# One core, a hybrid encoder block: one moving operand of 512 columns for both parts of h, and an adding transfer for the low part of some weights

## The chip, the cores and the metric

The kernel runs on one core of a Trainium2 chip. TensorE multiplies matrices into PSUM, whose eight banks hold 512 floats a partition; VectorE and ScalarE take results out of PSUM and do the elementwise work; POOL (GpSimd) does a little of it and can issue transfers; SP issues nearly all transfers. The metric is the time of one execution in microseconds on the device. Lower is better.

## The reference

The input x has 256 tokens of 2048 channels, all in float32. What is computed:

```python
h = rms_norm(x, g_pre)
proj = h @ w_in                      # 2048 x 10688: MLA, RWKV, z and gate columns
# MLA: low-rank q and kv, rotary, softmax attention over 8 heads
# RWKV-7: token shift, decays and rates, two scans (forward, backward), 16 heads of 64
u_mla  = (y_mla  * silu(z_mla))  @ w_br_mla
u_rwkv = (y_rwkv * silu(z_rwkv)) @ w_br_rwkv
merged = sigmoid(gate_mla) * u_mla + sigmoid(gate_rwkv) * u_rwkv
x = x + rms_norm(merged @ w_out, g_post)
```

The projection by `w_in` is the largest part: 16 blocks of 128 channels (k), 256 tokens, 10688 columns.

## The kernel before

**Split products.** TensorE takes the rounded type fp32r. To keep accuracy, both operands of a large product are split in a high part (rounded) and a low part (what rounding left). A product is then three matmuls: high weights by high h, high weights by low h, low weights by high h, all added in one PSUM bank. h is split once, at the start, into `hhi` and `hlo` (16 blocks of 256 columns each). Weights are split as they come.

**Chunks.** `dma_stream` loads the weights through SP in chunks of 128 x 1024 floats (512 KB: four blocks k by 256 columns) into one of three buffers `raws`. `split_stream` makes the parts: ScalarE copies `raw` to the rounded high part (line 327), VectorE subtracts (line 330) and writes the low part. There are three buffers of each (`NSPL = 3`), used in turn, so a chunk's split starts when the matmuls of the chunk three earlier are done. `mm_stream` issues the matmuls (lines 396 to 398 in `cm_task`). All matmuls of a chunk read weights as the stationary operand and h as the moving one.

**Tasks.** A projection task takes 256 columns: four chunks, two column tiles of 128, both in one PSUM bank. When its last chunk is done, an `end` generator evicts the bank: `mix` for r, k and v, `ev_z` for z, a tanh for the gates, a copy for the low-rank parts. There are 12 tasks for r, k, v, eight for z, eight gates of each branch, and four low-rank ones. Banks come from two pools, `DB` (three, for tasks) and `MB` (five, for all else).

**The scan** runs in four quads of heads. A quad's front (`front_k`, `front_v`, `front_d` for each direction) makes its operands, `chunks_of` solves and scans; each quad waits for the one before. Projection tasks are issued between its steps. After the last quad come the kv and q projections, attention, the branch projections (`um_task`, `ur_task`), and the output projection.

**Order.** The order of work on every engine is fixed when the program is built. Streams are generators that ask for an engine with a cost in microseconds (`yield ("P", cost, ready)`); a planner, `Streams.run`, grants them by estimated time and rank. The chip keeps this order on each engine, and semaphores keep the dependences. POOL's queue holds some memsets of the scan and the 16 small transfers of `front_d` (line 670).

Of the kernel before, what the change touches and what calls it, by code (L numbers as in the profile page):

```python
# [35 lines left out]
RK = 2  # L36
WARM = 12

KEEP, KEEP2 = 6, 9
# [115 lines left out]
def encoder_block_kernel(  # L155
# [51 lines left out]
    ss, rs = sb([128, 2], "ss"), sb([128, 2], "rs")  # L207
    hhi, hlo = sb([128, KT, S], "hhi", dt=F32R), sb([128, KT, S], "hlo", dt=F32R)
    raws = [sb([128, 1024], f"raw{i}") for i in range(NRAW)]
# [3 lines left out]
    W = Free(works[:-1])  # L213
    MB = Free(pps.tile([128, 512], F32, tag=f"m{i}", bufs=1, name=f"m{i}") for i in range(5))
    DB = Free(pps.tile([128, 512], F32, tag=f"d{i}", bufs=1, name=f"d{i}") for i in range(3))
    yr = sb([128, 8, 256], "yr")
# [45 lines left out]
    def add_task(parts, begin, end, ready=None, again=None):  # L262


        t = (len(chunks), len(parts), begin, end, ready, again)
        for p in parts:
            c = Chunk()
            c.load, c.pairs, c.steps = p
            c.t = c.at = 0.0
            chunks.append(c)  # L270
        tasks.append(t)
# [38 lines left out]
    def split_stream():  # L310
        i = 0
        while True:
            yield ("W", lambda: i < done["dma"])
            c = chunks[i]
            raw, c.hi, c.lo, t = raws[i % NRAW], whis[i % NSPL], wlos[i % NSPL], c.t
            if i < hold["first"]:
                yield ("W", lambda: i < done["mm"] + NSPL)
                t = max(c.t, chunks[i - NSPL].end if i >= NSPL else 0.0)
            else:
                c.hi, c.lo = hold["take"](i - hold["first"])  # L320
            beside = [p for p in c.pairs if len(p) > 3]
# [12 lines left out]
            c.at = e  # L334
            i += 1
            done["split"] = i
# [34 lines left out]
    def cm_task(src, nk, xhi, xlo, mt, wd, end, kc=4, load_fn=None, ready=None, kready=None, k_first=0,  # L371
                begin=None, pairs=None, first_alone=False):

        parts = []
        nb = (len(mt) + 1) // 2
        k0s = list(range(k_first, nk, kc))
        if first_alone:
            k0s[1:1] = [1]
        for i, k0 in enumerate(k0s):
            kc = (k0s + [nk])[i + 1] - k0  # L380

            def load(raw, k0=k0, kc=kc):
                if load_fn:
                    load_fn(raw, k0, kc)
                else:
                    nc.sync.dma_start(raw[:, 0:kc * wd].rearrange("p (k c) -> p k c", k=kc), src[:, k0:k0 + kc])

            steps = []
            for k in range(k0, k0 + kc):
                def mm(banks, hi, lo, k=k, k0=k0, kc=kc):  # L390
                    hi = hi[:, 0:kc * wd].rearrange("p (k c) -> p k c", k=kc)[:, k - k0]
                    lo = lo[:, 0:kc * wd].rearrange("p (k c) -> p k c", k=kc)[:, k - k0]
                    for i, (c, m) in enumerate(mt):
                        o = p2(banks[i // 2])[0:m, i % 2]
                        last = k == nk - 1 and (i % 2 == 1 or i == len(mt) - 1)
                        pe.matmul(o, hi[:, c:c + m], xhi(k), start=k == k_first and i % 2 == 0, stop=False)  # L396
                        pe.matmul(o, hi[:, c:c + m], xlo(k), start=False, stop=False)  # L397
                        pe.matmul(o, lo[:, c:c + m], xhi(k), start=False, stop=last)  # L398

                steps.append((len(mt) * 3 * 0.119, mm) + (((lambda k=k: kready(k)),) if kready else ()))  # L400
            parts.append((load, list(pairs(k0, kc)) if pairs else plain(kc * wd), steps))

        def take():
            b = []
            for _ in range(nb):
                b.append((yield from DB.take()))
            return b

        add_task(parts, begin or take, end, ready)
# [56 lines left out]
    def ev_second(b):  # L466
        yield ("W", lambda: len(have.get("part", ())) == 2)
        for p, m, t, B in zip(b, (96, 128), have["part"], (DB, MB)):
            yield ("D", cD(512))
            tt(w2d(t)[0:m], w2d(t)[0:m], p2(p)[0:m], ALU.add)  # L470
            B.give(p)
        yield from ev_wd(have["part"][0])
        yield from ev_ad(have["part"][1])
# [37 lines left out]
    def rwkv_tasks(Q, **kw):  # L511
        for n, nm in ((1, "k"), (0, "r"), (2, "v")):
            def end(b, n=n, nm=nm):
                t = yield from W.take(KEEP)
                yield from mix(p2(b[0]), 128, V_MU + 8 * n + 2 * Q, w2d(t))
                DB.give(*b)
                have[nm, Q] = t
            in_task(RW0 + 1024 * n + 256 * Q, end, **kw)

    def ev_z(b, o):  # L520

        z = p2(b[0])
        t = yield from W.take()
        yield ("A", cA(512), None, "exp")
        act.activation(w2d(t), z, AF.Tanh, scale=0.5)
        yield ("D", cD(512))
        stt(o, w2d(t), 1.0, z, ALU.add, ALU.mult)
        W.give(t)
        DB.give(*b)

# [7 lines left out]
    def gate_mla_task(g):  # L538
        def end(b):
            yield ("A", cA(512), None, "exp")  # L540
            act.activation(m16[:, 2 * g:2 * g + 2], p2(b[0]), AF.Tanh, scale=0.5)
            DB.give(*b)
        in_task(GM0 + 256 * g, end)

    def low_rank_task(c0, key):
        def end(b):
            t = yield from W.take(KEEP)
            yield ("A", cA(512))
            act.copy(w2d(t), p2(b[0]))
            DB.give(*b)  # L550
            have[key] = t
# [107 lines left out]
    def front_d(Q, d):  # L659
# [7 lines left out]
        raw = krw[d] if Q == 0 else (yield from W.take())  # L667
        e = yield ("G", 2.1, O.free["P"] if Q == 0 else None)
        for i, w in enumerate(((w2_f, a2_f), (w2_b, a2_b))[d]):
# [373 lines left out]
    def wkv_task(g):  # L1043
        wkv_v = wkv_b.rearrange("(k p) c -> p k c", p=128)

        def begin():
            if g == 0:
                yield ("W", lambda: quads[3].done and len(MB.tiles) > 1)
                DB.give(MB.tiles.pop())
                att["kT"] = sb([128, 2, 8, 256], "g16", dt=F32R)  # L1050
# [11 lines left out]
            a = yield from DB.take()  # L1062
            b = yield from DB.take()
            return a, b

# [37 lines left out]
    def wq_task(g):  # L1103
        wq_v = wq_b.rearrange("(k p) (h c) -> p k h c", p=128, c=192)

        def begin():
            a = yield from DB.take()
            b = yield from DB.take()
            return a, b

# [46 lines left out]

        add_task(parts, begin, end, lambda: have["qhl"][1] if "qhl" in have else None)

# [91 lines left out]
    def gate_rwkv_task(g):  # L1251
# [22 lines left out]

        in_task(GR0 + 256 * g, end)

# [34 lines left out]
    def out_task(n, wo_v=w_out.rearrange("(k p) c -> p k c", p=128)):  # L1311
        N = slice(512 * n, 512 * n + 512)

        def begin():
            if n == 0:
# [3 lines left out]
                MB.tiles.clear()  # L1319
            a = yield from DB.take()  # L1320
            b = yield from DB.take()
            return a, b

# [30 lines left out]
        def gain(b, t):  # L1354
            yield ("D", cD(512))
            tt(fin["og"][:, t, N], b[t], fin["gpb"][:, N], ALU.mult)
            DB.give(b[t])

        def end(b):
            for t in range(2):  # L1360
                yield from square(b, t)
                yield from gain(b, t)
            fin["left"] -= 2
            if n == 2:
# [159 lines left out]

    def begin_second():
        a = yield from DB.take()
        b = yield from MB.take()
        return a, b
# [3 lines left out]
    cm_task(None, KT, *HX, LORA, 512, ev_second, kc=2, pairs=pairs_first, load_fn=load_first, kready=lambda k: have.get(("h", k)),  # L1532
            k_first=UN, begin=begin_second)
    rwkv_tasks(0, kready=lambda k: have.get(("h", k)))
# [119 lines left out]
```

## Time and profile before

| | |
|---|---|
| median of 3 runs | 873.82 us (873.45 to 874.61) |
| the profiled execution | 872.72 us, its span 870.9 |
| TensorE busy | 848.3 us (97%) |
| VectorE busy | 659.3 us (76%) |
| ScalarE busy | 501.1 us (58%) |
| POOL busy | 30.7 us (4%) |
| DMA queue of SP | 135.16 MB, 52.4% of 16 engines' span |

The span runs from the first to the last instruction of one profiled execution; what lies around it is 1.8 us. Busy times are of that execution alone. Matmuls overlap in the pipeline, so that the durations of single matmuls add up to more than TensorE's busy time: from one start to the next is what a matmul takes of the stream.

### The profile page before, as it was taken

To read this page: it belongs to the slowest core of one execution; us is meant where nothing else is said; L and a number is where in the kernel's file an instruction comes from. 1 tells how busy PE (TensorE), PEld (TensorE's weight loads), DVE (VectorE), ACT (ScalarE), POOL (GpSimd) and SP (SyncE) were. 2 spreads that over 40 slices of the span, in tenths; PEclk is the share of its full clock that TensorE was granted. 3 is DMA by queue.
4 is the path that set the end of the run, shared out by engine and by line. 5 is a ranking of instruction groups with operands and counts; after the bars stand their busy time and mean duration, and the time that the engine had idled before them with its cause. 6 is when DMAs were issued, how large, how long until landed. Compare 5 with 4: busy or idle time off the path is not lost.

```text
span 870.9 us, 19398 instructions
## 1 busy us (share of the span) xinstructions
PE 848.3 (97%) x8112; PEld 810.0 (93%) x8112; DVE 659.3 (76%) x1082; ACT 501.1 (58%) x797; POOL 30.7 (4%) x66
## 2 busy tenths in 40 slices
PE   9999999999999999999999999999999999999996
PEld 8999999988899998999889999899999999998884
DVE  5878898868987878988789878775867556775554
ACT  6777644487544578354776445586766434444442
POOL 4110000000000000000000000000000000000000
PEclk9999999999999999999999999999999999999999
DMA  9565646633376523565423665346444675555553
GB/s 286 169 181 148 176 129 187 169 99 90 101 212 177 161 68 97 158 193 169 132 76 96 195 188 152 98 149 186 136 128 147 232 257 190 176 193 193 194 195 119
DMA packets 123528, 139.41 MB, mean 160 GB/s; under 512 B 6704, under 2 KB 110512, under 8 KB 123056
## 3 DMA queue, kind: packets, MB, share of 16 engines
q1 hardware_dynamic: 121664, 135.16, 52.4%
q0 software_dynamic: 768, 1.57, 0.6%
q10 hardware_dynamic: 1008, 1.44, 0.5%
q8 instruction: 63, 1.03, 0.5%
q14 instruction: 25, 0.20, 0.1%
HBM read 136.05 MB, written 2.10 MB: 159 GB/s over the span
## 4 chain that ended last, share of the span: by engine, by line
PE 73%; DVE 14%; ACT 8%; issue 2%; DMA 2%; DVEq 0%; ACTq 0%
PE d L396 16%; PE d L398 16%; PE d L397 15%; DVE wlo L330 4%; PE m L1334 2%; PE m L1335 2%; PE m L1336 2%; ACT whi L327 2%; DVE work L191 2%; PE m L398 2%; PE m L396 2%; PE m L397 2%; PE d L1335 1%; PE d L1334 1%; PE d L1336 1%
## 5 line engine op out<-in xcount | busy, mean ns | idle before, releaser
L327 ACT CAST whi<-raw 128x1024 fp32r<-128x1024 f32 (+3 forms) x252 | 252.8, 1004 | 254.2 <-PE d L397 155.1
L330 DVE TENSOR_TENSOR wlo<-raw,whi 128x1024 fp32r<-128x1024 f32 (+3 forms) x250 | 292.4, 1171 | 125.0 <-ACT whi L327 123.4
L396 PE MATMUL d<-hhi,whi 128*128 128x256 f32 (+1 forms) x1296 | 375.1, 289 | 0.0
L398 PE MATMUL d<-hhi,wlo 128*128 128x256 f32 (+1 forms) x1296 | 366.5, 283 | 2.3 <-DVE wlo L330 2.3
L397 PE MATMUL d<-hlo,whi 128*128 128x256 f32 (+1 forms) x1296 | 366.2, 283 | 0.0
L396 PEld LDWEIGHTS d<-hhi,whi 128*128 128x128 f32 (+1 forms) x1296 | 246.8, 190 | 4.5
L398 PEld LDWEIGHTS d<-hhi,wlo 128*128 128x128 f32 (+1 forms) x1296 | 246.9, 190 | 2.7 <-DVE wlo L330 2.7
L397 PEld LDWEIGHTS d<-hlo,whi 128*128 128x128 f32 (+1 forms) x1296 | 247.1, 191 | 0.1
L191 DVE TENSOR_TENSOR work<-work,work 128x512 f32<-128x512 f32 (+5 forms) x64 | 38.8, 612 | 3.9 <-ACT work L575 1.2
L191 DVE TENSOR_TENSOR u<-u,tmp 128x30 f32<-128x30 f32 (+7 forms) x120 | 29.9, 250 | 3.0
L191 DVE TENSOR_TENSOR tmp<-u 128x30 f32<-128x30 f32 (+7 forms) x120 | 29.8, 249 | 2.9
L396 PE MATMUL d<-b,whi 128*128 128x256 f32 x96 | 27.1, 282 | 0.0
L398 PE MATMUL d<-b,wlo 128*128 128x256 f32 x96 | 27.1, 282 | 0.0
L398 PE MATMUL d<-ar,wlo 128*128 128x256 f32 x96 | 27.0, 281 | 0.0
L397 PE MATMUL d<-work,whi 128*128 128x256 f32 x96 | 26.9, 280 | 0.0
L397 PE MATMUL d<-ar,whi 128*128 128x256 f32 x96 | 26.9, 280 | 0.0
L396 PE MATMUL d<-ar,whi 128*128 128x256 f32 x96 | 26.8, 279 | 0.0
L1334 PE MATMUL m<-whi,hhi 128*128 128x512 f32 x60 | 23.3, 389 | 0.0
L1335 PE MATMUL m<-wlo,hhi 128*128 128x512 f32 x60 | 23.3, 389 | 0.0
L1336 PE MATMUL m<-whi,hlo 128*128 128x512 f32 x60 | 23.3, 389 | 0.0
L191 DVE TENSOR_TENSOR g<-m,mask 128x512 f32<-128x512 f32 x32 | 20.6, 686 | 0.0
L797 PE MATMUL m<-ar,u 64*128 64x128 f32 x256 | 19.2, 285 | 0.3 <-DVE g L191 0.3
(334 smaller groups left out, 1487.3 us busy)
## 6 DMA issues: line engine op xcount, KB each, us to landing
raw<-in_w_in_dram SPq DMA_DIRECT2D x160, 512.0 KB, 3.9
raw<-in_w_out_dram SPq DMA_DIRECT2D x32, 512.0 KB, 3.6
raw<-in_w_br_mla_dram SPq DMA_DIRECT2D x16, 512.0 KB, 4.0
raw<-in_w_br_rwkv_dram SPq DMA_DIRECT2D x16, 512.0 KB, 3.3
raw<-in_mla_wkv_b_dram SPq DMA_DIRECT2D x8, 512.0 KB, 3.9
raw<-in_mla_wq_b_dram SPq DMA_DIRECT2D x8, 384.0 KB, 3.3
raw<-in_w_in_dram SPq DMA_DIRECT2D x7, 384.0 KB, 5.3
g<-in_x_dram SPq DMA_DIRECT2D x2, 1024.0 KB, 6.9
```

What stands on the lines that cost most here:

```text
L191: dve.tensor_tensor(out=o, in0=a, in1=b, op=op)
L327: act.copy(dst(c.hi), src(raw))
L330: eng.tensor_tensor(out=dst(c.lo), in0=src(raw), in1=dst(c.hi).bitcast(F32), op=ALU.subtract)
L396: pe.matmul(o, hi[:, c:c + m], xhi(k), start=k == k_first and i % 2 == 0, stop=False)
L397: pe.matmul(o, hi[:, c:c + m], xlo(k), start=False, stop=False)
L398: pe.matmul(o, lo[:, c:c + m], xhi(k), start=False, stop=last)
L797: pe.matmul(m[:, q * 128:q * 128 + 128], z.kb[R64[h], d, j, q], z.ar[d][R64[h], j, q], start=q == 0, stop=q == 3)
L1334: pe.matmul(banks[t], hhi[:, k, T], hi, start=k == 0, stop=False)
L1335: pe.matmul(banks[t], hhi[:, k, T], lo, start=False, stop=False)
L1336: pe.matmul(banks[t], hlo[:, k, T], hi, start=False, stop=k == KT - 1)
```

## The change

`hhi` and `hlo` become the two halves of one tile `hh`. In 32 of the projection tasks the high weights then meet both halves in one matmul of 512 columns, which fills a bank, and the low weights meet the high half in one of 256 columns, which adds into the bank's first half. Each column tile has a bank of its own, so a task takes two, and its eviction first adds the halves (`total`). The eight recurrent gates (`both=None`), the low-rank starts, and all products behind them keep the three matmuls. The pools become four and four banks.

In one chunk of three (`i % 3 == 1`), from the end of quad 0's second front until quad 3 is done, ScalarE writes the negated rounded weights to the low part, POOL issues a transfer that adds the weights from DRAM to it, and ScalarE writes the high part; VectorE does nothing for that chunk. The planner counts the transfer as landing 4.0 us after its issue, and gives the next load on SP 1.46 us for it.

```diff
+ACC, LAND = 3, 4.0
...
-    hhi, hlo = sb([128, KT, S], "hhi", dt=F32R), sb([128, KT, S], "hlo", dt=F32R)
+
+    hh = sb([128, 2, KT, S], "hh", dt=F32R)
+    hhi, hlo = hh[:, 0], hh[:, 1]
...
-    MB = Free(pps.tile([128, 512], F32, tag=f"m{i}", bufs=1, name=f"m{i}") for i in range(5))
-    DB = Free(pps.tile([128, 512], F32, tag=f"d{i}", bufs=1, name=f"d{i}") for i in range(3))
+    MB = Free(pps.tile([128, 512], F32, tag=f"m{i}", bufs=1, name=f"m{i}") for i in range(4))
+    DB = Free(pps.tile([128, 512], F32, tag=f"d{i}", bufs=1, name=f"d{i}") for i in range(4))
+
+    def take_banks(n):
+        b = []
+        for _ in range(n):
+            b.append((yield from DB.take()))
+        return b
...
             for (n, src, dst, *_) in c.pairs[:len(c.pairs) - len(beside)]:
+                if c.again and i % ACC == 1 and ("front", 0, 1) in have and not quads[3].done:
+
+                    e = yield ("A", cA(n), t)
+                    act.activation(dst(c.lo), src(raw), AF.Copy, scale=-1.0)
+                    e = yield ("G", 0.65, e)
+                    c.again(c.lo)
+                    O.free["S"] = max(O.free["S"], O.free["G"]) + 1.46
+                    yield ("A", cA(n), t)
+                    act.copy(dst(c.hi), src(raw))
+                    e += LAND
+                    continue
...
+            def again(lo, k0=k0, kc=kc):
+                gp.dma_start(lo[:, 0:kc * wd].rearrange("p (k c) -> p k c", k=kc), src[:, k0:k0 + kc], accum_op=ALU.add)
...
                     for i, (c, m) in enumerate(mt):
+                        if both:
+
+                            o = p2(banks[i])[0:m]
+                            pe.matmul(o, hi[:, c:c + m], both(k), start=k == k_first, stop=False)
+                            pe.matmul(o[:, 0], lo[:, c:c + m], xhi(k), start=False, stop=k == nk - 1)
+                            continue
...
-                steps.append((len(mt) * 3 * 0.119, mm) + (((lambda k=k: kready(k)),) if kready else ()))
...
+                steps.append((len(mt) * (0.347 if both else 3 * 0.119), mm) + (((lambda k=k: kready(k)),) if kready else ()))
...
     def in_task(c0, end, w=256, mt=PAIR, **kw):
+        kw.setdefault("both", lambda k: hh[:, :, k])
         cm_task(w_in_v[:, :, c0:c0 + w], KT, *HX, mt, w, end, **kw)
+
+    def total(b, o):
+
+        for i in range(2):
+            yield ("A", cA(256) - 0.05)
+            act.copy(o[:, i], p2(b[i])[:, 1])
+        for i in range(2):
+            yield ("D", cD(256))
+            tt(o[:, i], p2(b[i])[:, 0], o[:, i], ALU.add)
+            DB.give(b[i])
...
                 t = yield from W.take(KEEP)
-                yield from mix(p2(b[0]), 128, V_MU + 8 * n + 2 * Q, w2d(t))
-                DB.give(*b)
+                yield from total(b, w2d(t))
+                yield from mix(w2d(t), 128, V_MU + 8 * n + 2 * Q, w2d(t))
...
-        z = p2(b[0])
+        yield from total(b, o)
...
-            act.activation(m16[:, 2 * g:2 * g + 2], p2(b[0]), AF.Tanh, scale=0.5)
-            DB.give(*b)
+            act.activation(o, o, AF.Tanh, scale=0.5)
...
-            yield ("A", cA(512))
-            act.copy(w2d(t), p2(b[0]))
-            DB.give(*b)
+            yield from total(b, w2d(t))
...
-        in_task(GR0 + 256 * g, end)
+        in_task(GR0 + 256 * g, end, both=None)
```

## Rows read from the trace of the kernel before

**Rows 1.** The page: span, busy time of each engine, and the granted clock in 40 slices.

```profile
span 870.9 us, 19398 instructions
PE 848.3 (97%) x8112; PEld 810.0 (93%) x8112; DVE 659.3 (76%) x1082; ACT 501.1 (58%) x797; POOL 30.7 (4%) x66
PEclk9999999999999999999999999999999999999999
```

**Rows 2.** The page: shares of the chain that ended last, by engine and by line.

```profile
PE 73%; DVE 14%; ACT 8%; issue 2%; DMA 2%; DVEq 0%; ACTq 0%
PE d L396 16%; PE d L398 16%; PE d L397 15%; DVE wlo L330 4%; PE m L1334 2%; PE m L1335 2%; PE m L1336 2%; ACT whi L327 2%; DVE work L191 2%; PE m L398 2%; PE m L396 2%; PE m L397 2%; PE d L1335 1%; PE d L1334 1%; PE d L1336 1%
```

**Rows 3.** Busy time by engine, summed over 88 to 558 us (stretch, then engines).

```profile
sum 470.00, PE 459.86 PEld 441.65 DVE 397.90 ACT 273.81 POOL 12.80; mean PE 51.10 PEld 49.07 DVE 44.21 ACT 30.42 POOL 1.42
```

**Rows 4.** Timeline of TensorE in the projection: start, us, line, op, tiles.

```profile
639.81 0.28 PE L397 MATMUL d<-hlo,whi 128*128 128x256 f32 x1
643.89 0.28 PE L398 MATMUL d<-hhi,wlo 128*128 128x256 f32 x1
```

**Rows 5.** Timeline of TensorE in the output projection.

```profile
799.78 0.39 PE L1334 MATMUL m<-whi,hhi 128*128 128x512 f32 x1
805.90 0.39 PE L1334 MATMUL d<-whi,hhi 128*128 128x512 f32 x1
```

**Rows 6.** Groups by line: shapes, count | busy us, mean ns | idle before.

```profile
L396 PE MATMUL d<-hhi,whi 128*128 128x256 f32 (+1 forms) x1296 | 375.1, 289 | 0.0
L1086 PE MATMUL d<-whi,b 128*128 128x256 f32 x32 | 9.0, 281 | 0.0
```

**Rows 7.** The split's subtraction, 88 to 558 us: count, ns least/median/most.

```profile
L330 DVE TENSOR_TENSOR wlo<-raw,whi x124: 1201/1225/1228, 87.6 to 555.1; 128x1024 fp32r<-128x1024 f32 x124
```

**Rows 8.** Groups by line and shape: ScalarE's cast, VectorE's subtraction.

```profile
L327 ACT CAST whi<-raw 128x1024 fp32r<-128x1024 f32 x227 | 238.0, 1049 | 247.2 <-PE d L397 155.1 <-PE d L1336 24.5 <-DMA raw<-in_w_in_dram 15.1
L330 DVE TENSOR_TENSOR wlo<-raw,whi 128x1024 fp32r<-128x1024 f32 x227 | 277.5, 1224 | 114.4 <-ACT whi L327 112.7
```

**Rows 9.** POOL's own transfers: duration of an issue in ns, and issue to landing.

```profile
L670 POOL DMA_DIRECT2D work<-in_rwkv_w_f_dram x4: 512/512/645, 17.5 to 351.6; - x4
DMA to landing us min/median/max: 2.1/3.1/4.8
```

**Rows 10.** Timeline of ScalarE in a steady stretch.

```profile
497.20 1.05 ACT L327 CAST whi<-raw 128x1024 fp32r<-128x1024 f32 x1 [1.83 <-PE d L397]
500.08 1.05 ACT L327 CAST whi<-raw 128x1024 fp32r<-128x1024 f32 x1 [1.83 <-PE d L397]
```

**Rows 11.** The subtraction's instructions alone, by stretch; DMA share, GB/s at the end.

```profile
118.00:176.00 58.00, 24.48 (x21) 0.00 (x0) 1.00 0.63 174
248.00:298.00 50.00, 20.82 (x17) 0.00 (x0) 1.00 0.65 182
364.00:418.00 54.00, 22.02 (x18) 0.00 (x0) 1.00 0.65 183
486.00:536.00 50.00, 20.99 (x18) 0.00 (x0) 1.00 0.65 180
```

**Rows 12.** Weight loads issued by one line: us from issue to landing.

```profile
DMA to landing us min/median/max: 3.1/3.8/6.3
```

**Rows 13.** Transfers by issue: count, KB each, median us to landing.

```profile
raw<-in_w_in_dram SPq DMA_DIRECT2D x160, 512.0 KB, 3.9
g<-in_x_dram SPq DMA_DIRECT2D x2, 1024.0 KB, 6.9
yr<-in_g_post_dram SPq DMA_DIRECT2D x1, 1024.0 KB, 4.8
work<-in_rwkv_w_f_dram POOLq DMA_DIRECT2D x4, 96.0 KB, 2.8
```

**Rows 14.** Groups by line and shape: 256 columns out of PSUM.

```profile
L1205 ACT COPY work<-m 128x256 f32<-128x256 f32 x16 | 5.8, 377 | 1.8 <-PE m L1203 1.8
L191 DVE TENSOR_TENSOR tmp<-m,z 128x256 f32<-128x256 f32 x8 | 3.4, 425 | 1.1 <-PE m L941 0.9
```

More of the change, by code (lines that the diff above doesn't have):

```diff
@@ L267, in add_task @@
             c = Chunk()
-            c.load, c.pairs, c.steps = p
+            c.load, c.pairs, c.steps, c.again = *p, *([None] * (4 - len(p)))
             c.t = c.at = 0.0
@@ L371, in cm_task @@
     def cm_task(src, nk, xhi, xlo, mt, wd, end, kc=4, load_fn=None, ready=None, kready=None, k_first=0,
-                begin=None, pairs=None, first_alone=False):
+                pairs=None, first_alone=False, both=None):
         parts = []
-        nb = (len(mt) + 1) // 2
         k0s = list(range(k_first, nk, kc))
@@ L398, in mm @@
                         pe.matmul(o, lo[:, c:c + m], xhi(k), start=False, stop=last)
-                steps.append((len(mt) * 3 * 0.119, mm) + (((lambda k=k: kready(k)),) if kready else ()))
[L401 to L409, printed above, removed]
+                steps.append((len(mt) * (0.347 if both else 3 * 0.119), mm) + (((lambda k=k: kready(k)),) if kready else ()))
+            parts.append((load, list(pairs(k0, kc)) if pairs else plain(kc * wd), steps, None if load_fn else again))
+        add_task(parts, lambda: take_banks(len(mt) if both else (len(mt) + 1) // 2), end, ready)
     HX = (lambda k: hhi[:, k]), (lambda k: hlo[:, k])
@@ L467, in ev_second @@
         yield ("W", lambda: len(have.get("part", ())) == 2)
-        for p, m, t, B in zip(b, (96, 128), have["part"], (DB, MB)):
+        for p, m, t in zip(b, (96, 128), have["part"]):
             yield ("D", cD(512))
             tt(w2d(t)[0:m], w2d(t)[0:m], p2(p)[0:m], ALU.add)
-            B.give(p)
+            DB.give(p)
         yield from ev_wd(have["part"][0])
@@ L520, in ev_z @@
     def ev_z(b, o):
-        z = p2(b[0])
+        yield from total(b, o)
         t = yield from W.take()
         yield ("A", cA(512), None, "exp")
-        act.activation(w2d(t), z, AF.Tanh, scale=0.5)
+        act.activation(w2d(t), o, AF.Tanh, scale=0.5)
         yield ("D", cD(512))
-        stt(o, w2d(t), 1.0, z, ALU.add, ALU.mult)
+        stt(o, w2d(t), 1.0, o, ALU.add, ALU.mult)
         W.give(t)
-        DB.give(*b)
     def z_task(c0, key):
@@ L539, in end @@
         def end(b):
+            o = m16[:, 2 * g:2 * g + 2]
+            yield from total(b, o)
             yield ("A", cA(512), None, "exp")
-            act.activation(m16[:, 2 * g:2 * g + 2], p2(b[0]), AF.Tanh, scale=0.5)
-            DB.give(*b)
+            act.activation(o, o, AF.Tanh, scale=0.5)
         in_task(GM0 + 256 * g, end)
@@ L547, in end @@
             t = yield from W.take(KEEP)
-            yield ("A", cA(512))
-            act.copy(w2d(t), p2(b[0]))
-            DB.give(*b)
+            yield from total(b, w2d(t))
             have[key] = t
@@ L667, in front_d @@
         raw = krw[d] if Q == 0 else (yield from W.take())
-        e = yield ("G", 2.1, O.free["P"] if Q == 0 else None)
+        e = yield ("G", 1.2, O.free["P"] if Q == 0 else None)
         for i, w in enumerate(((w2_f, a2_f), (w2_b, a2_b))[d]):
@@ L1047, in begin @@
             if g == 0:
-                yield ("W", lambda: quads[3].done and len(MB.tiles) > 1)
-                DB.give(MB.tiles.pop())
+                yield ("W", lambda: quads[3].done)
                 att["kT"] = sb([128, 2, 8, 256], "g16", dt=F32R)
@@ L1061, in begin @@
                     tt(t[R64[i]], kr[R64[i]], att["kr"][0][R64[i]].bitcast(F32), ALU.subtract)
-            a = yield from DB.take()
-            b = yield from DB.take()
-            return a, b
+            return (yield from take_banks(2))
         parts = []
@@ L1104, in wq_task @@
         wq_v = wq_b.rearrange("(k p) (h c) -> p k h c", p=128, c=192)
[L1106 to L1109, printed above, removed]
         parts = []
@@ L1156, in end @@
                 O.add(head(g, i), 1, O.free["D"])
-        add_task(parts, begin, end, lambda: have["qhl"][1] if "qhl" in have else None)
+        add_task(parts, lambda: take_banks(2), end, lambda: have["qhl"][1] if "qhl" in have else None)
     def half_split(src, hi, lo, n):
@@ L1319, in begin @@
                 MB.tiles.clear()
-            a = yield from DB.take()
-            b = yield from DB.take()
-            return a, b
+            return (yield from take_banks(2))
         parts, more = [], []
@@ L1356, in gain @@
             tt(fin["og"][:, t, N], b[t], fin["gpb"][:, N], ALU.mult)
-            DB.give(b[t])
         def end(b):
@@ L1362, in end @@
                 yield from gain(b, t)
+                DB.give(b[t])
             fin["left"] -= 2
@@ L1523, in pairs_first @@
                ("kr", 0 if k0 < 2 else 2 if k0 < 8 else 8))
[L1525 to L1528, printed above, removed]
     LORA = [(0, 96), (128, 96), (256, 128), (384, 128)]
@@ L1532, in encoder_block_kernel @@
     cm_task(None, KT, *HX, LORA, 512, ev_second, kc=2, pairs=pairs_first, load_fn=load_first, kready=lambda k: have.get(("h", k)),
[L1533 removed]
+            k_first=UN)
     rwkv_tasks(0, kready=lambda k: have.get(("h", k)))
```

## The prediction, made before the changed kernel was run

> **What bounds the kernel now.** I read the page's busy times first, then the chain that ended last, then the engines in stretches of the span. TensorE is busy for 848.3 of the 870.9 us and holds its upper clock, 2.4 GHz, in every slice [rows 1]; the chain is 73% TensorE, and the three lines of the projection's matmuls carry most of it [rows 2]. So a microsecond off TensorE's own stream counts nearly whole, and one taken off VectorE or ScalarE counts only where TensorE waits for it. Between 88 and 558 us, which is where the scan of the four quads runs, TensorE is busy for 459.86 of 470 us [rows 3]: at most 10.1 us of waiting can be won there. VectorE has 397.90 us in it (85%), ScalarE 273.81 (58%).
>
> **Part 1, the long moving operand.** Today each (k, column tile) of a projection is three matmuls of 256 columns; afterwards it is one of 512 and one of 256. What counts is start to start, since the durations in the profile overlap. In the projection, 34 steps lie between the two rows at 639.81 and 643.89 us: 4.08/34 = 0.1200 us each [rows 4]. In the output projection the matmuls have 512 columns: 27 steps from 799.78 to 805.90 us, 6.12/27 = 0.2267 us [rows 5]. At 2.4 GHz these are 288 and 544 cycles: the columns and 32 more, whatever the length. A group thus goes from 3 x 0.1200 = 0.3600 to 0.2267 + 0.1200 = 0.3467 us, 13.3 ns less. The change reaches 32 tasks (12 for r, k, v; 8 gates of the attention branch; 8 z; 4 low rank) x 16 k x 2 tiles = 1024 groups. The eight recurrent gates keep the old form, 8 x 32 = 256 groups, and the two low-rank starts their 64; together these are 1344, of which 1296 stand in the first row of [rows 6] and the rest write banks of the other pool. Term: 1024 x 13.3 ns = **-13.65 us**, all on TensorE's stream. A moving operand in two pieces (the two halves lie apart in SBUF) is to be seen in the kv projection, where two runs of 128 columns cost a mean of 281 ns against 289 for the plain one [rows 6], so I charge nothing for the stride. Bounds: 0, if each half pays the 32 cycles again, and 13.65.
>
> The Trainium skill speaks against this term: "TensorE: Matmul & The Clock Gate", section "Back-to-back issue gap", gives N/2.4 + 2.5 ns at the full clock, so only 2.5 ns a matmul could be saved by joining two. By it the term would be 1024 x 2.5 ns = -2.6 us; the 13.3 ns that this trace shows over the columns [rows 4, 5] disagree, and I go by the trace.
>
> **Part 2, the adding transfer.** For one chunk in three, from the end of the first front to the end of the last quad, ScalarE writes the negated rounded weights into the low tile, POOL issues a transfer that adds the weights from DRAM, and ScalarE then writes the high part. Between 88 and 558 us 124 chunks are split [rows 7], so some 41 are taken. Removed: 41 VectorE subtractions of 1.224 us = 50 us. Added: 41 ScalarE passes of 1.049 us = 43 us [rows 8], and 41 issues on POOL of 0.512 us, the duration of its small transfers there [rows 9], 21 us on an engine that is busy for 30.7 of 870.9 [rows 1]. More descriptors may make an issue longer than that.
>
> What TensorE feels is when the low part is ready. There are three buffers of split weights. A cast starts when the matmuls of the chunk three earlier end, and in the steady stretches every 2.88 us [rows 10]: that is one chunk of 24 matmuls at 0.1200. From the cast's start TensorE still has two chunks to do. After the change a chunk is 8 x 0.3467 = 2.77 us, so the first low matmul is due 2 x 2.77 + 0.23 (its high matmul) = 5.77 us after ScalarE starts. ScalarE's pass takes 1.05, and I allow 0.1 for the hand-overs, which leaves **4.6 us** from POOL's issue to landing. Today the subtraction takes 1.2 of it. That tight spacing holds in four stretches with 21 + 17 + 18 + 18 = 74 chunks in 212 us [rows 11], 25 of them with an adding transfer. The other 50 chunks are spread over 258 us (5.2 us each), so their 16 transfers have some 9 us and cost nothing.
>
> How long the adding transfer takes, no row shows. From below: the 512 KB weight loads, in the same runs of 1 KB, land in 3.1/3.8/6.3 us (least, median, most) [rows 12, 13]; that is 0.8 us early, and costs 0. From above: such a transfer reads its bytes from two places, 1 MB in all, and the slowest 1 MB load took 6.9 us [rows 13], which is 2.3 us late, 25 x 2.3 = 58 us. The other 1 MB load, issued amid the branch projections' weight loads, took 4.8 us [rows 13]. I take that one: same size, same company. It is 0.2 us late, 25 x 0.2 = **+5.0 us**. The gain of part 1 is gone at 13.65/25 = 0.55 us late, that is at 5.15 us to landing. POOL's own small transfers (96 KB [rows 13]) take 2.1/3.1/4.8 us [rows 9], so the fixed part on that queue is no shorter than on SP's.
>
> The Trainium skill's "DMA: Bandwidth & Descriptors", section "Anatomy of one DMA", puts a transfer from POOL's queue at 2.0 us plus its bytes at 436 GB/s. That would be an estimated 3.2 us for 512 KB and 4.4 for 1 MB, both inside the 4.6, and the stall would be 0; the 96 KB rows at a median of 3.1 [rows 9] are above what the rule gives them (2.2), so I don't rely on it.
>
> The extra 41 x 0.5 MB share the 16 DMA engines with the weight loads, which keep them 63 to 65% busy in the tight stretches [rows 11]. A weight load has some 6 us (three chunks, 8.3 us, less about 2.1 until ScalarE has read the buffer twice) against a median of 3.8, so it stays covered; it costs if a load's time grows by half. On POOL the issues stand in one queue with the memsets of the scan's tiles, which wait for a tile's last reader, and an issue behind one is late by that wait. Those memsets belong to the scan's wide stretches, where the transfer has its 9 us: 0, unless such a wait passes 4 us.
>
> **Part 3, banks and evictions.** A task now fills two banks, and the two halves are summed on the way out: 2 ScalarE copies of 256 columns at 0.377 us and 2 VectorE additions at 0.425 [rows 14], for 32 tasks 24 us on ScalarE and 27 on VectorE. TensorE covers them: four banks are two tasks, so the eviction has the 11.1 us of the next task for 1.6 us of work. Should that cover go, each late eviction stalls TensorE by what it is late; behind it in ScalarE's and VectorE's queues stand the next chunk's split and the scan's steps. The scan has four banks in place of five. VectorE ends with 50 - 27 = 23 us less, ScalarE with 43 + 24 = 67 us more (58% becomes 73% of those 470 us). Both ways this acts only through the 10.1 us of waiting: it can give back at most that, and I let it cost as much at the other end. I take 0, since one engine gains about where the other loses.
>
> **Sum.** The profiled execution took 872.72 us (span 870.9 and 1.8 around it): 872.72 - 13.65 + 5.0 + 0 = 864.1. The median of the runs shown, 873.82, is 1.1 above it, so I forecast **865.2 us**.
>
> **Rivals.** (a) *The transfer lands late.* The adding transfer moves twice the bytes and meets weight loads that already hold the DMA engines 65% [rows 11]; at 5.6 us it is 1.0 late, 25 us: 872.72 - 13.65 + 25 + 1.1 = 885. It decides from 5.15 us on. For it: the 6.9 us row, and single loads of 6.3 [rows 12, 13]. Against it: 3.8 in the median, and 4.8 for 1 MB. (b) *The join saves nothing*, each half paying its 32 cycles: 872.72 + 5.0 + 1.1 = 879. Against it: the kv projection's split operand [rows 6]. The skill's rule above points the same way, with most of the gain missing. (c) *The evictions eat it*: two banks a task and 15 points more on ScalarE cost the 10 us that I allowed: 865.2 + 8 to 10 = 873 to 875, about no change. For it: VectorE at 85% [rows 3], where the sums queue. (d) *Everything lands in time* (under 4.6 us), and a relieved VectorE gives back some 4 of the 10.1 us of waiting: 872.72 - 13.65 - 4 + 1.1 = 856.
>
> **How the numbers follow.** Forecast 0.48 (own range 860 to 870), (d) 0.14, (a) 0.22, (b) 0.06, (c) 0.10. 0.2% is 1.75 us, about what a measurement of this kernel can tell from no change. Faster by more: 0.48 + 0.14 = 0.62, less 0.01 for the forecast's edge: 0.61. Within it: (c) for the most part, 0.10. Slower: (a) + (b) + the rest, 0.29. The range, 855 to 890, leaves out the lower edge of (d), about 0.05, and the part of (a) with landings past 5.8 us, about 0.12.
>
> **What would show it.** Part 1: the projection's matmuls step by 0.227 and 0.120 us, and 1024 of each stand in the groups. Part 2: some 42 transfers on POOL's queue into the low tiles; their median time to landing against 4.6 us, and TensorE idle before the low matmul, released by that transfer, at some 5 us in total (under 3 is (d), over 14 is (a)). Part 3: TensorE waits for VectorE's sums nowhere by more than a few us in total. The forecast is wrong if landings pass 5.15 us in the tight stretches, or if the 512-column step there is above 0.227.

## The result, and the profile after

The changed kernel takes **999.57 us** (median of 4 runs, 998.31 to 1000.71) against 873.63 of the kernel before, run beside it: a ratio of 1.144 [1.142, 1.146]. The forecast was 865.2, in a range to 890: faster was forecast and slower measured, and the time is off by 134 us.

The page, the answer to [rows 1]:

```profile
span 996.5 us, 17533 instructions
PE 887.8 (89%) x7088; PEld 785.5 (79%) x7088; DVE 639.1 (64%) x1109; ACT 553.5 (56%) x894; POOL 78.9 (8%) x103
PEclk9999988899988989998997988899999999999998
```

The span is 125.6 us longer. TensorE is idle for 996.5 - 887.8 = 108.7 us of the span, against 22.6 before: 86.1 more. It is also *busy* for 39.5 us more, with 1024 matmuls fewer. The line of clocks shows what goes with it: it was 9 in every slice, and now 8 stands in many, with a 7. The groups of instructions show where the idle time lies (to be held against [rows 6, 8, 9]):

```profile
L420 PE MATMUL d<-hh,whi 128*128 128x512 f32 x1024 | 400.1, 427 | 0.0
L421 PE MATMUL d<-hh,wlo 128*128 128x256 f32 x1024 | 305.6, 298 | 80.5 <-DMA wlo<-in_w_in_dram 78.3
L339 ACT ACTIVATE wlo<-raw 128x1024 fp32r<-128x1024 f32 x37 | 39.2, 1059 | 137.4 <-PE d L421 135.3
L409 POOL DMA_DIRECT2D wlo<-in_w_in_dram x37 | 47.9, 1295 | 508.6 <-ACT wlo L339 425.2
```

Of the 86.1 us, 80.5 stand before one line, the low weights' matmul, and 78.3 of these end with the adding transfer. The waits put that at 25 times, 4.7 us the longest:

```profile
PE d L421 <- DMA wlo<-in_w_in_dram: 78.3, 25, 4.7
```

The transfers by issue, from issue to landing (median), and the line's least, median and most, against [rows 12, 13]:

```profile
raw<-in_w_in_dram SPq DMA_DIRECT2D x160, 512.0 KB, 4.3
wlo<-in_w_in_dram POOLq DMA_DIRECT2D x37, 512.0 KB, 7.7
...
DMA to landing us min/median/max: 5.9/7.7/9.3
```

The adding transfer lands 7.7 us after its issue; not one lands within the 4.6 us that a steady stretch leaves. The timeline of TensorE around one such stall:

```profile
584.85 0.40 PE L420 MATMUL d<-hh,whi 128*128 128x512 f32 x1
...
586.97 0.40 PE L420 MATMUL d<-hh,whi 128*128 128x512 f32 x1
590.85 0.39 PE L421 MATMUL d<-hh,wlo 128*128 128x256 f32 x1 [3.48 <-DMA wlo<-in_w_in_dram]
591.07 0.40 PE L420 MATMUL d<-hh,whi 128*128 128x512 f32 x1
...
592.60 0.63 PE L420 MATMUL d<-hh,whi 128*128 128x512 f32 x1
593.02 0.41 PE L421 MATMUL d<-hh,wlo 128*128 128x256 f32 x1
593.24 0.63 PE L420 MATMUL d<-hh,whi 128*128 128x512 f32 x1
...
595.07 0.40 PE L420 MATMUL d<-hh,whi 128*128 128x512 f32 x1
...
600.72 0.40 PE L420 MATMUL d<-hh,whi 128*128 128x512 f32 x1
```

Before the stall, six groups take 2.12 us. After it, from 592.60 to 593.24, one takes 0.64, nearly twice as long: TensorE is at 1.2 GHz. It is back at 2.4 GHz at 595.07, from where 16 groups take 5.65 us, 0.353 each. The seven groups from 591.07 to 595.07 take 4.00 us in place of 2.47, so a stall of 3.5 us costs 1.5 us more behind it. Over the span the mean granted clock is 0.948, which is 0.052/0.5 x 996.5 = 104 us at the lower level, and half of it, at most 52 us, is work done late:

```profile
core 0: 996.5 us, clock 0.948
```

So the 125.6 us are +86.1 idle and +39.5 busy. The join takes some 7 off the busy time (below), which leaves 47 for the lower clock, under its bound of 52. That 47 is what is left over, not a measurement; two experiments below (the adding transfers alone, and the stalls filled) show 33 to 37 us of it.

### The profile page after: what moved, and what is told of

It is laid out like the page before. It is cut to its first block, busy times and chain, and to the rows that moved or that the text cites. A ratio compares the mean times of both kernels' runs of the same rounds, so it can differ in the third digit from the quotient of the medians.

```text
span 996.5 us, 17533 instructions
## 1 busy us (share of the span) xinstructions
PE 887.8 (89%) x7088; PEld 785.5 (79%) x7088; DVE 639.1 (64%) x1109; ACT 553.5 (56%) x894; POOL 78.9 (8%) x103
## 3 DMA queue, kind: packets, MB, share of 16 engines
q1 hardware_dynamic: 121664, 135.16, 45.4%
q0 software_dynamic: 20304, 20.97, 13.5%
## 4 chain that ended last, share of the span: by engine, by line
PE 38%; DMA 8%; ACT 4%; DVE 3%; issue 1%; POOL 0%; DVEq 0%; ACTq 0%
DMA wlo<-in_w_in_dram 6%; PE d L425 6%; PE d L427 5%; PE d L426 5%; PE d L420 3%; PE d L421 2%; PE m L1358 1%; PE m L1356 1%; PE m L1357 1%; PE d L1356 1%; PE d L1358 1%; PE d L1357 1%; ACT wlo L339 1%; DMA work<-in_rwkv_a_f_dram 1%; PE m L1236 1%
## 5 line engine op out<-in xcount | busy, mean ns | idle before, releaser
L420 PE MATMUL d<-hh,whi 128*128 128x512 f32 x1024 | 400.1, 427 | 0.0
L421 PE MATMUL d<-hh,wlo 128*128 128x256 f32 x1024 | 305.6, 298 | 80.5 <-DMA wlo<-in_w_in_dram 78.3
L351 DVE TENSOR_TENSOR wlo<-raw,whi 128x1024 fp32r<-128x1024 f32 (+3 forms) x213 | 247.4, 1162 | 193.3 <-ACT whi L348 192.5
L421 PEld LDWEIGHTS d<-hh,wlo 128*128 128x128 f32 x1024 | 210.0, 205 | 88.9 <-DMA wlo<-in_w_in_dram 86.4
L420 PEld LDWEIGHTS d<-hh,whi 128*128 128x128 f32 x1024 | 208.1, 203 | 49.3
L425 PE MATMUL d<-hh,whi 128*128 128x256 f32 (+1 forms) x320 | 93.0, 291 | 0.0
L427 PE MATMUL d<-hh,wlo 128*128 128x256 f32 (+1 forms) x320 | 90.5, 283 | 0.0
L426 PE MATMUL d<-hh,whi 128*128 128x256 f32 (+1 forms) x320 | 90.4, 282 | 0.0
L409 POOL DMA_DIRECT2D wlo<-in_w_in_dram x37 | 47.9, 1295 | 508.6 <-ACT wlo L339 425.2
L425 PEld LDWEIGHTS d<-hh,whi 128*128 128x128 f32 (+1 forms) x320 | 60.3, 188 | 0.9
L426 PEld LDWEIGHTS d<-hh,whi 128*128 128x128 f32 (+1 forms) x320 | 60.3, 189 | 0.1
L427 PEld LDWEIGHTS d<-hh,wlo 128*128 128x128 f32 (+1 forms) x320 | 60.3, 188 | 0.0
```

Source lines behind the costliest of these rows:

```text
L409: gp.dma_start(lo[:, 0:kc * wd].rearrange("p (k c) -> p k c", k=kc), src[:, k0:k0 + kc], accum_op=ALU.add)
L420: pe.matmul(o, hi[:, c:c + m], both(k), start=k == k_first, stop=False)
L421: pe.matmul(o[:, 0], lo[:, c:c + m], xhi(k), start=False, stop=k == nk - 1)
```

## The experiments

The order of work is planned anew for every kernel, so each experiment also moves work a little. Here is the same account for all of them, from each page: idle is span less TensorE's busy time, the last column is span x (1 - clock)/0.5. All columns but the median belong to the one profiled execution; with ScalarE's half it took 889.1 us, and with four split buffers 934.94.

| kernel | median us | span | idle | busy | mean clock | us at 1.2 GHz |
|---|---|---|---|---|---|---|
| before | 873.63 | 870.9 | 22.6 | 848.3 | 0.998 | 3 |
| changed | 999.57 | 996.5 | 108.7 | 887.8 | 0.948 | 104 |
| join alone | 915.30 | 912.7 | 54.2 | 858.5 | 0.963 | 68 |
| adding transfers alone | 990.01 | 986.3 | 101.4 | 884.9 | 0.954 | 91 |
| stalls filled | 978.73 | 976.4 | 45.8 | 930.6 | 0.987 | 25 |
| plain transfers | 904.80 | 900.8 | 45.4 | 855.4 | 0.987 | 23 |
| four split buffers | 919.50 to 936.71 | 933.2 | 62.0 | 871.2 | 0.964 | 67 |
| evictions added | 899.39 | 896.7 | 42.2 | 854.5 | 0.983 | 30 |
| ScalarE's half of them | 884.05 | 887.3 | 31.1 | 856.2 | 0.982 | 32 |
| two banks held | 875.31 | 873.7 | 24.4 | 849.3 | 0.998 | 3 |
| both of these | 912.68 | 911.5 | 49.6 | 861.9 | 0.975 | 46 |

**The adding transfers alone.** The kernel before with that hunk of the change; three matmuls a group, five and three banks.

```diff
+                    act.activation(dst(c.lo), src(raw), AF.Copy, scale=-1.0)
...
+                    c.again(c.lo)
```

> The kernel before with the adding transfers alone: three matmuls of 256 columns, five and three banks, old evictions. My theory: 873.6 + 25 stalls of 3.3 - 0.2 us (78) + what the clock loses (126 + 13.65 - 81 = 58) = 1009, between 995 and 1020. Rival (the join makes the stalls, since it shortens the cover by 0.2 us a chunk and takes a bank from the scan): under 950.

Measured: 990.01 (988.06 to 994.38), ratio 1.133 [1.130, 1.137], below the expected range. One line holds the idle time:

```profile
L414 PE MATMUL d<-hhi,wlo 128*128 128x256 f32 (+1 forms) x1296 | 384.5, 297 | 81.0 <-DMA wlo<-in_w_in_dram 80.2
```

The transfers alone make +116 us, by the same wait. The stalls came out as expected, and the miss is in the clock: TensorE is busy for 36.6 us more than before, with the same matmuls, where 58 had been expected.

**The transfers by themselves.** A kernel that does only transfers of 512 KB, four of each kind, here without the plain ones of SP and the plain ones in runs of 4 KB: plain from POOL, adding into float32, plain into the rounded type, adding into the rounded type, the same in runs of 4 KB, and adding beside 18 loads on SP's queue.

```diff
+        gp.dma_start(k4(t), short(n))
+        gp.dma_start(k4(t), short(n), accum_op=ALU.add)
+        gp.dma_start(k4(r), short(n))
+        gp.dma_start(k4(r), short(n), accum_op=ALU.add)
+        gp.dma_start(r, w[:, n, 0:1024], accum_op=ALU.add)
```

> Transfers alone, no other work (the output is not the reference's): 512 KB into one tile, four of each kind one after the other: SP plain, POOL plain, POOL adding into float32, POOL converting into fp32r, POOL adding into fp32r, POOL adding with runs of 4 KB, POOL plain with runs of 4 KB, and at last POOL adding into fp32r beside 18 weight loads on SP. My theory (the add itself is slow: 101 ns a packet of 1 KB against 46 plain, and a longer issue): adding lands in 5.9 us alone and 7 to 8 us beside loads, plain from POOL in about 4. Rival (only the company of the weight loads makes it late): under 4.6 us alone. Open, no forecast: whether the conversion or the addition costs it, and what longer runs do.

Measured, by line, in that order (duration of an issue, then issue to landing):

```profile
L95 POOL DMA_DIRECT2D plain<-in_w_in_dram x4: 748/760/919, 15.9 to 29.8; - x4
DMA to landing us min/median/max: 4.2/4.3/4.4
...
L97 POOL DMA_DIRECT2D plain<-in_w_in_dram x4: 1267/1284/1313, 34.3 to 53.0; - x4
DMA to landing us min/median/max: 5.9/5.9/6.1
...
L100 POOL DMA_DIRECT2D rounded<-in_w_in_dram x4: 740/748/767, 60.3 to 74.1; - x4
DMA to landing us min/median/max: 4.1/4.2/4.5
...
L102 POOL DMA_DIRECT2D rounded<-in_w_in_dram x4: 1258/1273/1293, 78.5 to 97.2; - x4
DMA to landing us min/median/max: 5.9/5.9/6.0
...
L104 POOL DMA_DIRECT2D rounded<-in_w_in_dram x4: 835/844/867, 103.4 to 120.9; - x4
DMA to landing us min/median/max: 5.5/5.5/5.8
...
L114 POOL DMA_DIRECT2D rounded<-in_w_in_dram x4: 1268/1278/1308, 144.0 to 171.4; - x4
DMA to landing us min/median/max: 8.0/9.0/9.8
```

The addition costs 1.6 to 1.7 us with nothing beside it (5.9 against 4.3 in float32, against 4.2 rounded), a third of that in the issue; rounding costs nothing (5.9 either way with the addition). The company of weight loads adds some 3 us (9.0 against 5.9), above the 7 to 8 that were expected; those loads landed in 7.4 us themselves, against 3.7 alone, so they stood closer than in the kernel. So 4.6 us was out of reach in any case.

**Plain transfers in the changed kernel.** The low part then holds the whole weight.

```diff
-    gp.dma_start(lo[...], src[:, k0:k0 + kc], accum_op=ALU.add)
+    gp.dma_start(lo[...], src[:, k0:k0 + kc])
```

> The changed kernel with the one word for the addition taken out of its transfers: POOL issues plain transfers of the same weights into the low part, in the same places and order (so the low part holds the whole weight). Alone, such a transfer landed in 4.2 us and its issue took 0.75, against 5.9 and 1.27 for the adding one. Theory (the addition makes the transfer late): landing at a median of 5 to 6, the 81 us of stalls before the low matmuls fall to 20 to 45, time 930 to 965. Rival (any second transfer beside the weight loads is late): landing 7 or more, time 985 to 1000.

Measured: 904.80 (900.25 to 907.54), ratio 1.034 [1.030, 1.038], 95 us faster than the changed kernel for one word:

```profile
L421 PE MATMUL d<-hh,wlo 128*128 128x256 f32 x1024 | 291.0, 284 | 18.7 <-DMA wlo<-in_w_in_dram 16.2
...
DMA to landing us min/median/max: 4.2/4.6/8.8
```

The landing falls to a median of 4.6 and is just the room; the stalls fall to 18.7. Landing, stalls and time all lie below the expected ranges, so the addition counts for more than I thought. The rival, that any second transfer is late, is out. The queues of POOL, in the changed kernel and in this one (packets, MB, share of 16 engines' span), show where:

```profile
q0 software_dynamic: 20304, 20.97, 13.5%
...
q0 software_dynamic: 20304, 20.97, 10.3%
```

For the same packets and bytes that is 0.135 x 16 x 996.5/20304 = 0.106 us a packet with the addition and 0.073 without. That 904.8 lies below the join alone, at 915, would fit VectorE's 37 subtractions less: the scan's last matmul ends at 571.7 us here and at 614.8 there.

**The stalls filled.** Before each of the 25 late matmuls stand matmuls by zero (5 to 39, from the length of the stall), so that TensorE isn't idle.

```diff
+                            for _ in range(now.pop("fill", 0)):
+                                pe.matmul(o[:, 0]..., hi[:, c:c + m], zero..., start=False, stop=False)
```

> The changed kernel, with matmuls by zeros put into the 25 stalls: ahead of the first low matmul of each chunk that waited, as many of 256 columns as fill its wait but 0.2 us. They add nothing to the result; the stalls stay as long. My theory (idle TensorE falls to 1.2 GHz and runs the next microseconds at half speed, worth some 50 to 60 us): 940 to 952 us and a mean granted clock over 0.99. Rival (the clock falls for another reason, or its loss hides in the stalls): within 5 us of 999.6.

Measured: 978.73 (978.18 to 980.31). The clock rose to 0.987, not to above 0.99, and only 21 us came back, which lies in neither range. The account shows both sides. TensorE's idle time fell by 62.9 us, its busy time rose by 42.8, and the zero matmuls take up to 79.7 of it:

```profile
L428 PE MATMUL d<-zero,whi 128*128 128x256 f32 x631 | 79.7, 283 | 0.0
```

So some 80 us of fill stand for 63 of waiting, 17 too many, and the other matmuls were busy for 79.7 - 42.8 = 37 us less (33 if a zero matmul counts 0.120 us). That is what the clock gave back; at 104 - 25 = 79 us fewer at 1.2 GHz its bound is 39. The time alone shows 21, since the fill was too long.

**Four split buffers.** The changed kernel with one buffer more of either part, 15 work tiles in place of 19, and 7.7 and 1.28 us as prices in the plan.

```diff
-NW, NRAW, NSPL = 19, 3, 3
+NW, NRAW, NSPL = 15, 3, 4
```

> The changed kernel with four buffers of split weights in place of three (four work tiles fewer, 15 in place of 19, to make room), and the order of the work written for an issue of 1.28 us and a landing of 7.7. A chunk more between cast and matmul is 2.77 us more room: 7.4 in place of 4.6. Theory (the stalls are the landing less the room): those before the low matmuls fall from 81 us to 5 to 20, the low clock goes with them, and VectorE's 50 us of relief shorten the scan against the join alone: 885 to 915. Rival (the transfers load the DMA engines and so make the weight loads late whatever the room, or fewer work tiles cost the scan): 930 or more.

Measured: 919.50 in one of four runs (clock 0.983) and 933.93 to 936.71 in the others (0.964 to 0.968), too wide apart for an interval. The profile is of one at 934.94.

```profile
L421 PE MATMUL d<-hh,wlo 128*128 128x256 f32 x1024 | 293.8, 287 | 20.8 <-DMA wlo<-in_w_in_dram 20.8
...
DMA to landing us min/median/max: 5.9/7.7/10.2
```

The same landing, a chunk more of room, and 20.8 us of stalls in place of 80.5, all in 11 waits: this bears out that the wait is the landing less the room. By the medians 25 x (7.7 - 7.4) = 7.5 us would be left; single landings took up to 10.2. The time came out above what was expected in all four runs. Whether the four work tiles cost the rest was not tried.

**The join alone.** The changed kernel without the transfers.

```diff
-ACC, LAND = 3, 4.0
+ACC, LAND = 1 << 20, 4.0
```

> The changed kernel without its adding transfers: every low part is made by VectorE again; the joined matmuls, the banks and the evictions stay. My theory (the late transfers and what they do to TensorE's clock are the whole loss, the join gives its 13.65 us): 873.6 - 13.65 = 860, between 857 and 864. Rival (two banks a task and the added eviction work cost as well): 870 or more, with TensorE idle before the projection's matmuls.

Measured: 915.30 (913.19 to 916.58), ratio 1.047 [1.044, 1.049]. My theory fell: a change that saves TensorE's work costs 41 us (874.36 beside it). The join does what it says, with less gain: in a steady stretch (ScalarE's casts, as in [rows 10])

```profile
127.57 1.05 ACT L348 CAST whi<-raw 128x1024 fp32r<-128x1024 f32 x1
130.39 1.05 ACT L348 CAST whi<-raw 128x1024 fp32r<-128x1024 f32 x1 [1.77 <-PE d L420]
```

a chunk takes 2.82 to 2.83 us and not 2.77, against 2.88 before: some 6 to 7 ns a group, about 7 us in all and not 13.65. But late in the scan TensorE has too little to do (stretch and its length, busy us of TensorE, its weight loads, VectorE, ScalarE, POOL, granted clock, DMA share, GB/s):

```profile
475.00:500.00 25.00, 18.26 (x154) 14.44 (x148) 16.93 (x27) 17.69 (x35) 3.11 (x7) 0.80 0.34 93
500.00:525.00 25.00, 15.80 (x78) 12.89 (x79) 14.10 (x21) 5.74 (x11) 0.00 (x0) 0.52 0.00 1
525.00:550.00 25.00, 25.00 (x190) 23.98 (x189) 19.37 (x39) 12.38 (x17) 0.00 (x0) 1.00 0.62 164
...
575.00:600.00 25.00, 14.99 (x282) 12.88 (x280) 15.53 (x23) 11.78 (x22) 0.00 (x0) 0.66 0.25 81
600.00:625.00 25.00, 17.91 (x279) 15.75 (x278) 16.84 (x36) 11.31 (x27) 0.61 (x2) 0.80 0.01 2
```

From 500 to 525 us hardly a byte is loaded, and TensorE is at 1.2 GHz for nearly all of it. From 483 to 518.57 us no projection chunk is worked on, only the scan's own matmuls, and then the first one has waited for VectorE:

```profile
518.57 0.80 PE L420 MATMUL d<-hh,whi 128*128 128x512 f32 x1 [5.67 <-DVE work L193]
```

That is the sum that empties a bank. Between 449.71 and 518.10 us VectorE makes no such sum, while two tasks are multiplied, the last of their matmuls at 483.00: they hold all four banks. The program's order has their evictions that late, behind steps of the scan; why it does was not tried. Either the added evictions, or the two banks a task, or both must have brought it about.

**Evictions added, without the join.** The kernel before, and in the 32 tasks:

```diff
+        for i in range(2):
+            act.copy(o[:, i], p2(b[0])[:, i])
+        for i in range(2):
+            tt(o[:, i], p2(b[0])[:, i], o[:, i], ALU.max)
```

> The kernel before (three matmuls a group, no adding transfer, five and three banks), with the eviction work of the change put into the same 32 tasks without the join: per task two ScalarE copies of 256 columns and two VectorE passes of 256 (a maximum of the bank with its copy, which leaves the values as they are), then on from the copy. 24 us more on ScalarE, 27 on VectorE. Theory A, the evictions are what made the join alone slow (915 and not 860): VectorE is busy for 85% of the scan, which has little slack, so the scan becomes longer and TensorE runs out of projection work before the scan ends: 890 to 915. Theory B, it is the two banks a task: within 6 us of before, 868 to 880.

Measured: 899.39 (897.34 to 901.97), ratio 1.029 [1.026, 1.032]: +25.7 us for passes of 21.3 us on ScalarE and 26.3 on VectorE, two engines that were not the bound. A similar picture, later:

```profile
550.00:575.00 25.00, 13.49 (x224) 11.97 (x224) 14.39 (x28) 9.14 (x17) 0.00 (x0) 0.66 0.21 64
...
567.37 0.58 PE L396 MATMUL d<-hhi,whi 128*128 128x256 f32 x1 [1.92 <-ACT u L1279]
```

The last quad's scan (its last matmul) ends at 597.9 us and not at 563.6. In the stretch the DMA share is 0.21, and TensorE is busy for 13.49 of 25 us: from 552.8 to 567.37 no projection matmul runs, and the next one has waited for ScalarE's tanh of a recurrent gate (line 1279). The program lets these gates be evicted when the last quad's solve is done, or when many work tiles are free; until then three of them fill the three banks. In the kernel before the first of these tanhs ran at 537.8 us, here at 566.7, after the later solve.

**ScalarE's half alone** (the two copies, no second loop).

> The kernel before, with only the ScalarE half of the added eviction work: in the same 32 tasks two ScalarE copies of 256 columns out of the bank (24 us in all), and no added VectorE pass. With both halves the kernel took 899.4, 25.7 us more than before. Theory: the price is VectorE's 27 us, since VectorE is busy for 85% of the scan and ScalarE for 58%: 872 to 880 here. Rival: the copies stand in ScalarE's queue ahead of the next chunk's cast and of the scan's steps, so that half or more of the price comes from them: 886 to 900.

Measured: 884.05 (882.55 to 889.1), ratio 1.012 [1.010, 1.014]: in neither range. ScalarE's copies make 10.6 us; the other 15 are the difference to both halves, since VectorE's passes alone were not tried. So neither engine pays for all of it.

**Two banks held, without the join.**

```diff
+    def two():
+        a = yield from DB.take()
+        return a, (yield from DB.take())
...
+            kw.setdefault("begin", two)
```

> The kernel before with four and four banks, where each of the 32 tasks takes two banks, fills one as before and gives both back after its eviction. No join, no more evictions. Theory A (evictions): within 6 us of before, 868 to 880. Theory B (banks: two tasks' worth in place of three, and four for the scan): 890 to 920, with TensorE waiting for banks before the scan ends.

Measured: 875.31 (874.12 to 876.91), ratio 1.0017 [1.0007, 1.0027]. Banks alone cost 1.6 us.

**Both, without the join.**

> Both at once, still without the join: two banks taken a task (four and four) and the added eviction work. It is the join alone (915.3) without what the join saves. Either theory: if the saved 13.65 us of TensorE's stream still counted there, 925 to 932; if that saving was lost to waiting, since the scan sets the end, 911 to 919. If both together cost far more than the two apart, it is their combination: an eviction that is late holds two of four banks.

Measured: 912.68 (910.98 to 915.0), ratio 1.044 [1.042, 1.046]. Two things follow. Together they cost 39 us, 12 more than the two apart. An eviction that comes late now keeps two of four banks: here too TensorE waits 6.35 us for VectorE's sum, at 512.67 us, and in the kernel with the evictions alone 1.3 us, once. And the join alone, which is this plus the join (and two small changes of the plan: POOL's small transfers are priced at 1.2 us and not 2.1, and the second low-rank start takes both banks from `DB`), takes 915.3: what the join saves on TensorE is worth nothing here. The scan's last matmul ends at 612.2 us in this kernel and at 614.8 in the join alone, and 299 and 298 us follow: the scan sets the end.

**The join after the scan.** Where the scan is over, TensorE sets the pace. The kernel before, with the join in the last four recurrent gates, or in all eight:

```diff
-        in_task(GR0 + 256 * g, end)
+        in_task(GR0 + 256 * g, end, **({'both': lambda k: hh[:, :, k]} if g in range(4,8) else {}))
```

> The kernel before with the join in the last four recurrent gate tasks alone, five and three banks, no adding transfer. These tasks run after the scan, where VectorE and ScalarE have time and TensorE sets the pace: 4 x 32 groups x 13.3 ns = 1.7 us off, 871.5 to 873 on 873.9. Rival (a task's two banks or its sums cost there too): 874 to 880.

> The same in all eight recurrent gate tasks, with four and four banks. Four of them run before the scan ends. If the sums cost only where VectorE is full: 8 x 32 x 13.3 ns = 3.4 us, 870 to 872.5. If the four within the scan cost what the join alone showed (55 us on 32 tasks, some 1.7 each): 877 to 882.

Measured: 876.29 (ratio 1.0022 [1.0009, 1.0035]) and 878.20 (1.0047 [1.0029, 1.0066]): no gain in either, and both in the range of the rival. In the first:

```profile
612.12 0.28 PE L399 MATMUL d<-hh,wlo 128*128 128x256 f32 x1
614.78 0.79 PE L398 MATMUL d<-hh,whi 128*128 128x512 f32 x1 [2.38 <-DVE work L192]
615.38 0.41 PE L399 MATMUL d<-hh,wlo 128*128 128x256 f32 x1
615.59 0.63 PE L398 MATMUL d<-hh,whi 128*128 128x512 f32 x1
```

The second column tile needs a bank that VectorE has not yet cleared: 2.4 us of waiting, and 1.2 GHz behind it, for a saving of 4 x 32 x 7 ns = 0.9 us. The same wait, 2.38 us, stands in the second. No version beat the kernel before.

## Why the prediction was wrong

**The step that failed** is in part 2: "I take that one: same size, same company. It is 0.2 us late, 25 x 0.2 = +5.0 us." The room of 4.6 us held, and so did the 25 tight chunks. The landing was 7.7 us and not 4.8: 25 x (7.7 - 4.6) = 78 us, and the wait is 78.3. So near a match of a sum of medians is in part chance. The row that I took was one plain load from SP; nothing in it adds, and POOL's issue takes a median of 1.28 us here, against the 0.512 of the small transfer that I carried over with a warning but no price. The upper bound, 6.9, was too low as well, since it too was a plain transfer. Rival (a) had the late landing and a third of the size. It put it down to twice the bytes beside busy DMA engines; a plain transfer in the same place and company lands in 4.6 us, so the addition is what is late, with packets that take 0.106 us in place of 0.073.

**A term that was missing**: the clock. I noted that it was at 2.4 GHz throughout [rows 1] and did not ask what holds it there. A stall of 3.5 us is followed by a stretch at half rate; that made, by what is left over, about 47 us of the 126, and filling the stalls gave 33 to 37 of them back. The Trainium skill describes just this, in "TensorE: Matmul & The Clock Gate", section "HAM oscillation — how this bites in real kernels": matmuls that wait for a transfer in each turn of a loop lose the clock again and again. The timeline above agrees, with 0.64 us for a group behind a stall against 0.353; I had not weighed it.

**Part 1** was right in kind, and twice too large: a group takes 0.353 us, not 0.3467, so 7 us and not 13.65. In the join alone (126 to 170 us) the step behind a matmul of 512 columns is 0.237 us and not 0.2267, over the 0.227 that the prediction named as a sign of being wrong; the one behind 256 columns is 0.117. Whether the operand in two pieces, for which I charged nothing, makes the difference was not tried; the row for it gave durations, and not steps from start to start. The Trainium skill's rule, 2.6 us by the prediction, was too small; the measurement lies between. The section gives that rule for an isolated matmul and says that in a stream with weight loads it under-counts at small N and over-counts at large N, which the prediction left out; here it under-counts at both, with 0.109 us against 0.1200 at 256 columns and 0.216 against 0.2267 at 512.

**Part 3** failed too: "TensorE covers them". I took the cover of one eviction, 11.1 us of the next task's matmuls, and did not ask about the scan, which shares VectorE and ScalarE with it. The limit of 10.1 us on either side was no limit: it bounds what can be won from waiting, not what can be lost. Evictions alone cost 25.7 us, with the banks 39, and in the join alone TensorE waits 5.67 us for one of VectorE's sums, which the prediction had as "nowhere by more than a few us". In the changed kernel this part cannot be told apart: the transfers alone take 990, and the join with its evictions adds 10 to that. That late evictions cost less while TensorE waits for transfers anyway would fit, but is not shown.

**What stays open**: why ScalarE's copies make 10 of the 25.7 us (that they delay the scan's steps was only argued), what VectorE's passes cost alone, and what holds the four-buffer kernel above the 885 to 915 that were expected.

## What to carry to other kernels

A transfer that replaces work on a busy engine has to be priced by a row of its own kind, with its issue and with the loads that will run beside it; where no row shows it, measure it alone first. Price a stall of TensorE with the stretch at the lower clock behind it. And before giving an engine at 85% more work because another engine "covers" it, look for the chain that it serves: where a scan has no filler work left, or none whose banks are free, its delay becomes idle time on TensorE.

## What the runs showed that I had not expected

- Adding from DRAM costs 1.6 to 1.7 us on 512 KB, and the issue on POOL grows from 0.76 to 1.28 us; in runs of 4 KB the issue is 0.84, yet the landing still 5.5, against 3.8 for a plain one.
- Company costs the adding transfer more than others: it lands in 5.9 us alone and in 7.7 in the changed kernel, where the weight loads went only from 3.9 to 4.3; the plain one from POOL went from 4.2 to 4.6.
- POOL's own transfers of 96 KB, which [rows 13] has at 2.8 us, take a median of 7.5 in the changed kernel, where they share POOL's queue with the adding ones.
- In both kernels with the join after the scan TensorE waited 2.38 us and then ran at 1.2 GHz: in one at once, in the other after some 0.9 us at 2.4 GHz.
